# A hybrid DeltaNet and mLSTM layer on one core: gate functions and four kinds of transposition are issued a piece of the weight stream later

## The chip, the cores and the metric

The kernel runs on one core of a Trainium2 chip. The metric is the device time of one execution in microseconds (us), given as the median of three executions. The engines are named as in the profile: PE is TensorE (its matmuls; PEld are its weight loads), DVE is VectorE, ACT is ScalarE, POOL is GpSimd, SP is the queue from which all DMA transfers of this kernel start. Each engine takes its instructions strictly in the order in which the program issued them.

## The reference

One layer over 256 tokens of width 2048, all in float32. Two recurrent branches run side by side on the same normalised input and are merged by a gate for each channel:

```
h = RMSNorm_pre(x) * (1 + scale) + shift              # scale, shift, gate from c W_ada
[gdn_qkv | gdn_a, gdn_b | gdn_z | ml_qk | ml_v | ml_i, ml_f | ml_o | ml_z | g_A | g_B] = h W_in
y_A = W_pA( RMSNorm_head(GatedDeltaNet(conv(q, k, v), decay, beta)) * silu(gdn_z) )
y_B = W_pB( sigmoid(ml_o) * RMSNorm_head(mLSTM(conv(q, k), v, i, f)) * silu(ml_z) )
out = (sigmoid(g_A) * y_A + sigmoid(g_B) * y_B) W_out
x <- x + gate * RMSNorm_post(out)
```

The DeltaNet branch has 32 value heads, the mLSTM branch 8 heads of width 256. Both recurrences are computed from matmuls over the whole 256 tokens and a triangular inverse.

## The kernel before, in words

**The stream.** All weights pass through one object, `Stream`. A unit is one tile `raw` of 128 x 2048 floats (1 MB), three of which are kept in a ring. A unit is used in two **pieces** of 1024 columns. For a piece, `prep_w` writes two parts, the high part `whi` (a cast on ACT, line 169) and the remainder `wlo` (a subtraction, line 170, on DVE here; early in the kernel some on POOL). Four buffers of each are there. `mm3` (line 223) then makes each product of three matmuls: high by high, high by low, low by high. In most of the kernel a piece is 12 matmuls with 512 columns, or 24 with 256.

`Stream.run` writes the order of the work for all engines by hand. For piece i it issues the preparation of piece i + 3 (`ahead` is 3), then the matmuls of piece i, then, where the piece closes a group, that group's `after`, and then one `side.step()`. So in the queues of ACT and DVE the cast and the subtraction of piece i + 3 stand ahead of anything that follows from piece i. The cast of piece i + 4 needs the buffer that piece i frees.

**Side.** Everything that isn't a weight product is written as a generator in `Side` and goes on by one `yield` in each step, that is once in each piece. `wait(n)` lets n steps pass. Generators of rank 0 go first in a step, then those of rank 1 and 2. Instructions that a generator issues in step i stand on PE behind the matmuls of piece i and ahead of those of piece i + 1. PE works in order, so a transposition whose input isn't ready holds up the next piece. Steps that need PSUM tiles (`gtile`, four of them) ask with `banks` or `free` whether the tiles are free, and pass a step where they aren't.

**The first stage** (`BLOCKS`) computes 14 groups of 512 output columns in passes over parts of the contraction, since the input isn't complete yet. Each pass adds into the tiles `part` in SBUF. The last of these passes (contraction parts 12 to 15) sums up all 14 groups, two pieces for each. Its `after` adds the two PSUM tiles of the group on DVE (line 409), then applies on ACT a sigmoid (groups 0 to 8, 10 and 12) or SiLU (9, 11 and 13) over 128 x 1024 values (line 418), and stores the result in DRAM (`gate_dr`, line 420). For the odd groups from 9 on, DVE first multiplies it with the group before (line 422; store in line 423). After the last group `branches_open` drains the side work and hands the memory of this stage to the branches.

**The small gates** (`gates`, lines 450 to 511) run as side work from the start of that last pass: exponentials, logarithms and scans over 128 x 256 values for decay, beta and the mLSTM's input and forget gates. At their end PE transposes the two tiles `gt` and `g2` (lines 507 and 508) and ACT and DVE copy the result.

**The DeltaNet branch** takes eight periods of two head pairs (`gdn_period`, `zg` from 0 to 7). At the end of each, `gdn_stage2` scales the output `on` on DVE (line 879), waits two steps and transposes it (line 888) for the store `o_dr`.

**The mLSTM branch** takes four pairs of heads (`mlstm`, `m` from 0 to 3). For pair 0 alone the output gates arrive late: `gated_by` multiplies `hn` with the SiLU gate on DVE (`gate`, line 1023), passes one step, and goes on in `mlstm_out`, whose transpositions are line 992. For the other pairs `gated` does it with gates from DRAM.

**The output.** In two halves of 1024 columns, both branches' projections are summed in `py` tiles, `merge` multiplies and adds them on DVE and POOL (lines 1180 and 1181) into the tile `mg`, passes one step, and transposes `mg` 256 columns at a time (line 1190) into `m_hi` and `m_lo`. After the second half it also loads the rows of the last scale (`rws`), writes their product to DRAM (`bg_dr`, line 1206), reads it back broadcast (`bg`, line 1210) and loads the residual `xr` (line 1213). The product with `w_out` (`pw` tiles) and the last norm follow.

Of the kernel before, what the change touches and what calls it, by code (L numbers as in the profile page):

```python
# [9 lines left out]
AF = mybir.ActivationFunctionType  # L10
ALU = mybir.AluOpType
# [106 lines left out]
def hybrid_layer_kernel(  # L118
# [25 lines left out]
    V, A, T, G, SP = nc.vector, nc.scalar, nc.tensor, nc.gpsimd, nc.sync  # L144
# [80 lines left out]
    side = Side()  # L225
# [155 lines left out]
    def branches_open():  # L381

        nonlocal bp, x0, y0
        side.drain()
        st.close()
        bp = br.enter_context(tc.tile_pool(name="bp", bufs=2))

        x0 = bp.tile([P, 8, P], F32, name="x0", tag="x0", bufs=1)
        y0 = bp.tile([64, 8, 64], F32, name="y0", tag="y0", bufs=1)
        G.memset(x0, 0.0)  # L390
        G.memset(y0, 0.0)

    def add_start_groups(bi):

        groups, k0, nk = BLOCKS[bi][:3]
        lastb = bi == len(BLOCKS) - 1

        def use(g, ps, c, hi, lo, o):

            k = k0 + c  # L400
            h_chunks(k)
            for b in range(2):
                mm3(ps[b], h_hi[:, k, b * P:(b + 1) * P], h_lo[:, k, b * P:(b + 1) * P],
                    hi[:, o:o + 512], lo[:, o:o + 512], c == 0, c == nk - 1)

        def after(g, ps):
            for b in range(2):
                if k0:
                    V.tensor_tensor(part[g][:, b], ps[b], part[g][:, b], op=ALU.add)  # L409
                elif bi or g < 4 or b == 0:  # L410
                    A.copy(part[g][:, b], ps[b])
                else:
                    V.tensor_copy(part[g][:, b], ps[b])
            if bi == len(BLOCKS) - 2 and g == 3:
                late_consts()
            if lastb:
                pt = part[g].rearrange("p b c -> p (b c)")
                A.activation(pt, pt, AF.Silu if g in (9, 11, 13) else AF.Sigmoid)
                if g < 8:
                    SP.dma_start(gate_dr[g], part[g])  # L420
                elif g % 2:
                    V.tensor_tensor(part[g], part[g], part[g - 1], op=ALU.mult)
                    SP.dma_start(gate_dr[8 + (g - 8) // 2], part[g])
                if g == NG - 1:
                    branches_open()

        adders = []
        per = 1 if nk > 2 else 2
        for g in groups[::per]:
            st_ = {}  # L430

            def use_piece(h, hi, lo, g=g, st_=st_):
                for i in range(min(2, per * nk - 2 * h)):
                    gg, c = g + (2 * h + i) // nk, (2 * h + i) % nk
                    if c == 0:
                        st_["ps"] = [jtile(f"pn{i}") for i in range(2)]
                    use(gg, st_["ps"], c, hi, lo, i * 512)
                    if c == nk - 1:
                        after(gg, st_["ps"])
                    if bi == 0 and gg == NE - 2:  # L440
                        h_chunks(1)
                stream.ahead = 3 if bi else 1
            src = tuple(w_in[START[g + i]][:, k0 * 512:(k0 + nk) * 512] for i in range(per))
            adders.append(lambda src=src, use_piece=use_piece:
                          stream.add(src, lambda h, raw: prep_w(h, raw, per * nk * 512), use_piece,
                                     (per * nk + 1) // 2))
        return adders


    def gates(ps):  # L450
        gp = sp
        work = sp.tile([P, 2, D], F32, name="work", tag="xs").rearrange("p b (n s) -> p (b n) s", s=S)
        used = []

        def t_(n):
            used.append(n)
            return work[:, len(used) - 1]
        xb, ab, e, u, l, r = (t_(n) for n in ("xb", "ab", "e", "u", "l", "r"))
        V.tensor_scalar(xb, ps[:, 0:S], late_c["abb"][:, 0:1], None, op0=ALU.add)
        yield  # L460
        A.activation(ab, xb, AF.Abs)
        A.activation(e, ab, AF.Exp, scale=-1.0)
        na = gp.tile([32, 1], F32, name="na")
        A.activation(na, late_c["alog"], AF.Exp)
        yield
        G.tensor_scalar(u, e, 1.0, None, op0=ALU.add)
        yield from wait(2)
        A.activation(l, u, AF.Ln)
        A.activation(r, l, AF.Exp, scale=-1.0)
        yield  # L470
        G.tensor_scalar(u, u, -1.0, None, op0=ALU.add)
        G.tensor_tensor(e, e, u, op=ALU.subtract)
        G.tensor_tensor(e, e, r, op=ALU.mult)
        G.tensor_tensor(l, l, e, op=ALU.add)
        mn, sp_ = ab, u
        gt, g2, zz, on_, bf, bm, mm_ = (t_(n) for n in ("gt", "g2", "zz", "on_", "bf", "bm", "mm_"))
        G.memset(gt, 0.0)
        G.memset(g2, 0.0)
        G.memset(zz, 0.0)
        G.memset(on_, 1.0)  # L480
        yield from wait(2)
        V.scalar_tensor_tensor(mn, xb, 0.0, l, op0=ALU.min, op1=ALU.subtract)
        V.scalar_tensor_tensor(sp_, xb, 0.0, l, op0=ALU.max, op1=ALU.add)
        yield
        V.tensor_scalar(sp_[0:32], sp_[0:32], na[:, 0:1], -1.0, op0=ALU.mult, op1=ALU.mult)
        V.tensor_tensor_scan(bf[96:104], on_[96:104], mn[96:104], 0.0, op0=ALU.mult, op1=ALU.add)
        SP.dma_start(bm[64:72], bf[96:104])
        yield
        for b in range(2):
            c0, c1 = b * P, (b + 1) * P  # L490
            V.tensor_tensor_scan(gt[0:32, c0:c1], on_[0:32, c0:c1], sp_[0:32, c0:c1], 0.0,
                                 op0=ALU.mult, op1=ALU.add)
        A.activation(gt[32:64], mn[32:64], AF.Exp)
        yield from wait(2)
        V.tensor_tensor(gt[64:72], xb[64:72], bm[64:72], op=ALU.subtract)
        V.tensor_tensor_scan(mm_[64:72], zz[64:72], gt[64:72], 0.0, op0=ALU.add, op1=ALU.max)
        yield
        V.tensor_tensor(bm[64:72], bm[64:72], mm_[64:72], op=ALU.add)
        V.tensor_scalar(mm_[64:72], mm_[64:72], -1.0, None, op0=ALU.mult)
        yield  # L500
        A.activation(g2[64:72], bm[64:72], AF.Exp, scale=-1.0)
        SP.dma_start(rows[0:32], gt[0:32])
        SP.dma_start(rows[32:40], mm_[64:72])
        yield from wait(2)
        tp = gtile("tp")
        for b in range(2):
            T.transpose(tp[:, b * P:(b + 1) * P], gt[:, b * P:(b + 1) * P], ident)
            T.transpose(tp[:, S + b * P: S + (b + 1) * P], g2[:, b * P:(b + 1) * P], ident)
        A.copy(tt.rearrange("p a b -> p (a b)"), tp[:, 0:S])
        A.copy(tte.rearrange("p a b -> p (a b)"), tp[:, S:2 * S])  # L510
        V.tensor_scalar(ngt, tt[:, :, 0:32], -1.0, None, op0=ALU.mult)
# [85 lines left out]
    def wait(n):  # L597
        for _ in range(n):
            yield
# [156 lines left out]
    def gdn_stage2(zg, res, zr):  # L756
# [116 lines left out]
        for g, z, h, c in heads:  # L873
# [4 lines left out]
            for blk in range(2):  # L878
                V.scalar_tensor_tensor(ons[z][:, blk, h], ons[z][:, blk, h], so[:, z, blk, h:h + 1], sz[:, blk, c],
                                       op0=ALU.mult, op1=ALU.mult)  # L880
        yield from wait(2)
        yield from free(4)
        pts = [gtile(f"pt{z}", True) for z in range(2)]
        side.debt -= 0.8
# [99 lines left out]
    def mlstm_out(m, r):  # L984
        while "hn" not in r:
            yield
        hn = r["hn"]
        for h in range(2):
            pt = gtile("mpt")
            for cc in range(2):  # L990
                for b in range(2):
                    T.transpose(pt[:, cc * S + b * P:cc * S + (b + 1) * P], hn[h][:, b, cc * P:(cc + 1) * P], ident)
            hT = bp.tile([P, 2, S], F32, name="hT", tag=("qh", "ql")[h], bufs=1)
            for cc in range(2):
                ch = (2 * m + h) * 2 + cc
                A.activation(hT[:, cc], pt[:, cc * S:(cc + 1) * S], AF.Copy, scale=late_c["mnw"][:, ch:ch + 1])
            ch = (2 * m + h) * 2
            SP.dma_start(hb_dr[ch:ch + 2].rearrange("c d t -> d c t"), hT)
            yield

    def mlstm(m):
# [29 lines left out]
        def gated_by(sg, first):  # L1031
            while "hn" not in r or not (first or "gated" in r):
                yield
            for b in range(2):
                gate(b, sg[:, b], first)
            r["gated"] = True
            yield
            if not first:
                yield from mlstm_out(m, r)

        def gated():
# [128 lines left out]
    def merge(hf, yb):  # L1170
# [11 lines left out]
            yield  # L1182
        if hf == 0:
            load_gates(1)
        yield
        for k2 in range(hf * 4, hf * 4 + 4):
            ps = gtile("mtp")
            for kk in range(2):
# [195 lines left out]
```

## Time and profile before

| | us |
|---|---|
| median of three executions | 1620.76 |
| lowest and highest | 1618.08, 1620.88 |
| the profiled execution | 1616.79 |
| its span, first to last instruction | 1615.0 |
| busy: PE, DVE, ACT, POOL | 1585.7, 1148.3, 936.4, 235.2 |

All rows below are from the profiled execution, with times from the start of its span. A matmul's row lasts longer than the distance to the next one, since matmuls are pipelined: matmuls with 512 columns follow each other after about 0.23 us, though each lasts 0.39. So what PE loses in a stall is read from the distance of two starts, and it is a little more than the idle time that the profile names. In the rows of the chain of waits the three numbers are the total, the number of waits and the longest. In a row of the timeline they are start, duration, and behind the row in brackets the idle time before it with what ended it.

### The profile page before, as it was taken

To read this page: it belongs to the slowest core of one execution; us is meant where nothing else is said; L and a number is where in the kernel's file an instruction comes from. 1 tells how busy PE (TensorE), PEld (TensorE's weight loads), DVE (VectorE), ACT (ScalarE), POOL (GpSimd) and SP (SyncE) were. 2 spreads that over 40 slices of the span, in tenths; PEclk is the share of its full clock that TensorE was granted. 3 is DMA by queue.
4 is the path that set the end of the run, shared out by engine and by line. 5 is a ranking of instruction groups with operands and counts; after the bars stand their busy time and mean duration, and the time that the engine had idled before them with its cause. 6 is when DMAs were issued, how large, how long until landed. Compare 5 with 4: busy or idle time off the path is not lost.

```text
span 1615.0 us, 25449 instructions
## 1 busy us (share of the span) xinstructions
PE 1585.7 (98%) x9844; PEld 1388.1 (86%) x9844; DVE 1148.3 (71%) x1798; ACT 936.4 (58%) x1497; POOL 235.2 (15%) x191
## 2 busy tenths in 40 slices
PE   7999999899999999999999999999999999999998
PEld 4888888689999999999999999889988788888886
DVE  6685555675689878887888888776778556756654
ACT  7744445664666575757666666664665544444443
POOL 1787761000000000000000000000010000100100
PEclk9999999999999999999999999999999999999999
DMA  9898775665555546454646464557778668767573
GB/s 375 342 408 334 263 286 191 236 244 204 181 182 191 183 170 193 171 191 158 205 159 197 157 196 169 184 211 246 281 291 315 222 247 293 280 233 250 196 275 115
DMA packets 96261, 372.37 MB, mean 231 GB/s; under 512 B 26262, under 2 KB 46214, under 8 KB 58252
## 3 DMA queue, kind: packets, MB, share of 16 engines
q1 hardware_dynamic: 96140, 370.75, 64.5%
q8 instruction: 77, 1.26, 0.3%
q14 instruction: 44, 0.36, 0.1%
HBM read 354.40 MB, written 16.31 MB: 230 GB/s over the span
## 4 chain that ended last, share of the span: by engine, by line
PE 88%; DVE 3%; ACT 3%; issue 2%; DMA 2%; POOL 1%; SPq 0%; DVEq 0%; POOLq 0%; ACTq 0%
PE pn L223 31%; PE pt L223 29%; PE py L223 16%; PE pw L223 5%; ACT whi L169 2%; DVE wlo L170 1%; DMA raw<-in_dram 1%; DVE part L409 1%; PE psa L223 1%; DMA ar<-in_dram 1%; PE mz L808 1%; PE mq L799 1%; PE po L848 0%; PE pa L820 0%; PE pc L838 0%
## 5 line engine op out<-in xcount | busy, mean ns | idle before, releaser
L170 DVE TENSOR_TENSOR wlo<-raw,whi 128x1024 fp32r<-128x1024 f32 x454 | 560.6, 1245 | 266.6 <-ACT whi L169 265.4
L169 ACT CAST whi<-raw 128x1024 fp32r<-128x1024 f32 (+1 forms) x517 | 532.1, 1046 | 314.3 <-PE pn L223 148.8
L223 PE MATMUL pt<-h_hi,whi 128*128 128x256 f32 x1280 | 368.8, 288 | 0.0
L223 PE MATMUL pt<-h_hi,wlo 128*128 128x256 f32 x1280 | 363.0, 284 | 0.0
L223 PE MATMUL pt<-h_lo,whi 128*128 128x256 f32 x1280 | 362.8, 283 | 0.0
L223 PE MATMUL pn<-whi,h_hi 128*128 128x512 f32 x896 | 354.2, 395 | 7.9 <-ACT whi L169 5.8
L223 PE MATMUL pn<-wlo,h_hi 128*128 128x512 f32 x896 | 351.1, 392 | 3.3 <-DVE wlo L170 2.5
L223 PE MATMUL pn<-whi,h_lo 128*128 128x512 f32 x896 | 349.9, 390 | 0.0
L223 PEld LDWEIGHTS pt<-h_hi,whi 128*128 128x128 f32 x1280 | 246.0, 192 | 1.4
L223 PEld LDWEIGHTS pt<-h_lo,whi 128*128 128x128 f32 x1280 | 246.2, 192 | 0.3
L223 PEld LDWEIGHTS pt<-h_hi,wlo 128*128 128x128 f32 x1280 | 246.0, 192 | 0.0
L223 PEld LDWEIGHTS pn<-whi,h_hi 128*128 128x128 f32 x896 | 168.7, 188 | 45.7 <-ACT whi L169 6.2
L223 PEld LDWEIGHTS pn<-wlo,h_hi 128*128 128x128 f32 x896 | 168.7, 188 | 41.6 <-DVE wlo L170 7.4
L223 PEld LDWEIGHTS pn<-whi,h_lo 128*128 128x128 f32 x896 | 168.5, 188 | 35.3
L170 POOL TENSOR_TENSOR wlo<-raw,whi 128x1024 fp32r<-128x1024 f32 (+1 forms) x63 | 146.1, 2327 | 67.2 <-ACT whi L169 65.0
L223 PE MATMUL py<-whi,yhi 128*128 128x512 f32 x384 | 150.6, 392 | 0.0
L223 PE MATMUL py<-whi,ylo 128*128 128x512 f32 x384 | 149.6, 390 | 0.0
L223 PE MATMUL py<-wlo,yhi 128*128 128x512 f32 x384 | 149.5, 389 | 0.0
L409 DVE TENSOR_TENSOR part<-pn,part 128x512 f32<-128x512 f32 x112 | 73.5, 685 | 52.4 <-PE pn L223 52.4
L169 ACT CAST yhi<-ya 128x512 fp32r<-128x512 f32 x48 | 29.9, 622 | 131.7 <-PE py L223 129.0
L170 DVE TENSOR_TENSOR ylo<-ya,yhi 128x512 fp32r<-128x512 f32 x48 | 33.2, 691 | 91.3 <-ACT yhi L169 89.5
L585 DVE SCALAR_TENSOR_TENSOR qs<-pt,gcv,qs 128x255 f32<-128x255 f32 (+2 forms) x192 | 92.1, 480 | 4.6
(244 smaller groups left out, 1785.2 us busy)
## 6 DMA issues: line engine op xcount, KB each, us to landing
raw<-in_dram SPq DMA_DIRECT2D x259, 1024.0 KB
ar<-in_dram SPq DMA_DIRECT2D x32, 1024.0 KB
raw<-in_dram SPq DMA_DIRECT2D x16, 512.0 KB
ya<-o_dr SPq DMA_DIRECT2D x32, 256.0 KB
gate_dr<-part SPq DMA_DIRECT2D x11, 512.0 KB
gb<-rows SPq DMA_DIRECT2D x20, 256.0 KB
raw<-in_dram SPq DMA_DIRECT2D x6, 768.0 KB
ug<-ud SPq DMA_DIRECT2D x32, 128.0 KB
```

The source lines that it names most:

```text
L169: A.copy(hi, src)
L170: (eng or V).tensor_tensor(lo, src, hi.bitcast(F32), op=ALU.subtract)
L223: T.matmul(ps, l, r, start=start and i == 0, stop=stop and i == 2, skip_group_check=True)
L409: V.tensor_tensor(part[g][:, b], ps[b], part[g][:, b], op=ALU.add)
L585: V.scalar_tensor_tensor(dst[:, n, sh:], src[:, 0:S - sh], taps(n, 3 - sh), dst[:, n, sh:], op0=ALU.mult, op1=ALU.add)
L799: T.matmul(psp[64:128, m * 64:(m + 1) * 64], um(m)[0:64, 64:128], y0[:, m], start=True, stop=True)
L808: T.matmul(psz[0:64, m * 64:(m + 1) * 64], p2[64:128, m], x0[64:128, m, 64:128], start=True, stop=True)
```

## The change

Five steps are issued later, nothing is added or removed:

- The function (line 418), store and product of a group of the last summed pass move out of `after` into a generator `gate_values` of rank 0. The function comes one piece later (with the store, for groups 0 to 7), the product and its store two pieces later. For the last group `branches_open` drains the generator at once.
- `gates`: three steps instead of two before the transpositions of `gt` and `g2`.
- `gdn_stage2`: three steps instead of two before the transpositions of `on`, where `zg // 7` is 1, so for `zg` 7 alone.
- `gated_by`: one more step before `mlstm_out`, for pair 0 of the mLSTM.
- `merge`: two steps instead of one before the transpositions of `mg`, in both halves.

```
@@ add_start_groups, after
             if lastb:
-                pt = part[g].rearrange("p b c -> p (b c)")
-                A.activation(pt, pt, AF.Silu if g in (9, 11, 13) else AF.Sigmoid)
-                if g < 8:
-                    SP.dma_start(gate_dr[g], part[g])
-                elif g % 2:
-                    V.tensor_tensor(part[g], part[g], part[g - 1], op=ALU.mult)
-                    SP.dma_start(gate_dr[8 + (g - 8) // 2], part[g])
+                side.add(gate_values(g), 0)
                 if g == NG - 1:
                     branches_open()
+
+        def gate_values(g):
+
+            yield
+            pt = part[g].rearrange("p b c -> p (b c)")
+            A.activation(pt, pt, AF.Silu if g in (9, 11, 13) else AF.Sigmoid)
+            if g < 8:
+                SP.dma_start(gate_dr[g], part[g])
+            elif g % 2:
+                yield
+                V.tensor_tensor(part[g], part[g], part[g - 1], op=ALU.mult)
+                SP.dma_start(gate_dr[8 + (g - 8) // 2], part[g])
@@ gates
         SP.dma_start(rows[32:40], mm_[64:72])
-        yield from wait(2)
+        yield from wait(3)
         tp = gtile("tp")
@@ gdn_stage2
-        yield from wait(2)
+        yield from wait(2 + zg // 7)
         yield from free(4)
         pts = [gtile(f"pt{z}", True) for z in range(2)]
@@ gated_by
             r["gated"] = True
             yield
             if not first:
+                yield
                 yield from mlstm_out(m, r)
@@ merge
         if hf == 0:
             load_gates(1)
-        yield
+        yield from wait(2)
         for k2 in range(hf * 4, hf * 4 + 4):
             ps = gtile("mtp")
```

## The prediction

> **What bounds the kernel now.** I began with the page of the profile, then took the chain of waits of PE.
>
> ```profile
> PE 1585.7 (98%) x9844; PEld 1388.1 (86%) x9844; DVE 1148.3 (71%) x1798; ACT 936.4 (58%) x1497; POOL 235.2 (15%) x191
> ```
>
> ```profile
> PE pn L223 <- DVE wlo L170: 2.5, 6, 0.6
> PE mpt L992 <- DVE hn L1023: 1.8, 2, 1.5
> PE pn L223 <- DVE part L409: 1.6, 3, 0.7
> PE tp L508 <- ACT work L501: 1.1, 1, 1.1
> PE pt L888 <- DVE on L879: 0.7, 1, 0.7
> PE mtp L1190 <- POOL mg L1181: 0.6, 1, 0.6
> ```
>
> PE is busy for 98% of the span, so only what stalls PE is worth anything. The change moves the waiting side of most of these rows. Next I put a size on the stalls of the last summed pass. The windows give its balance, the rows of the tiles `pab` and `pt` say when PE ends the product before it and begins the one behind it, and the timeline gives one piece.
>
> ```profile
> 260.00:355.00 95.00, 90.12 (x421) 71.97 (x420) 59.42 (x72) 65.36 (x71) 5.65 (x10) 1.00 0.61 221
> ...
> L223 PE MATMUL pab<-h_hi,wlo x16: 280/283/284, 257.1 to 263.5; 128*128 128x256 f32 x16
> ...
> L223 PE MATMUL pt<-h_hi,whi x1280: 277/283/472, 348.2 to 1222.1; 128*128 128x256 f32 x183
> ...
> 269.08 0.39 PE L223 MATMUL pn<-whi,h_hi 128*128 128x512 f32 x1
> ...
> 271.80 0.39 PE L223 MATMUL pn<-whi,h_hi 128*128 128x512 f32 x1
> ```
>
> A piece takes 271.80 - 269.08 = 2.72 us. The pass has 28 of them: 76.2 us. It begins at 263.6 and ends where `pt` begins, at 348.2, so it takes 84.6. Four transpositions of the small gates belong to it, estimated at 0.4 from the 1.04 us of eight (a row further below). **The pass loses 84.6 - 76.2 - 0.4 = 8.0 us.** DVE (59 of 95 us) and ACT (65 of 95) aren't full in it, so it isn't their amount of work but its order. ACT and DVE show how it comes about:
>
> ```profile
> 275.94 1.06 ACT L418 ACTIVATE part<-part 128x1024 f32<-128x1024 f32 x1 [2.68 <-DVE part L409]
> 277.02 1.28 ACT L468 ACT_TABLE_LOAD   x1
> ...
> 278.75 1.28 ACT L469 ACT_TABLE_LOAD   x1
> ...
> 280.37 1.99 ACT L169 CAST whi<-raw 128x1024 fp32r<-128x1024 f32 x2
> ...
> 281.43 2.94 DVE L170 TENSOR_TENSOR wlo<-raw,whi 128x1024 fp32r<-128x1024 f32 x2 [5.53 <-ACT whi L169]
> 284.30 1.27 DVE L409 TENSOR_TENSOR part<-pn,part 128x512 f32<-128x512 f32 x2
> ...
> 319.36 1.06 ACT L418 ACTIVATE part<-part 128x1024 f32<-128x1024 f32 x1 [2.49 <-DVE part L409]
> ...
> 324.98 1.06 ACT L418 ACTIVATE part<-part 128x1024 f32<-128x1024 f32 x1 [2.67 <-DVE part L409]
> ...
> 321.39 2.36 DVE L170 TENSOR_TENSOR wlo<-raw,whi 128x1024 fp32r<-128x1024 f32 x2 [2.06 <-ACT whi L169]
> 323.67 1.28 DVE L409 TENSOR_TENSOR part<-pn,part 128x512 f32<-128x512 f32 x2
> ```
>
> Pieces are numbered from 0, so piece 2 begins at 269.08 and, with no stall, piece i ends at 266.3 + 2.72 i. At 277.02 the small gates put two functions with two table loads on ACT, and the two casts behind them start only at 280.37. These are pieces 7 and 8. The adds of group 2 (pieces 4 and 5, ended at 279.9) stand on DVE behind the subtraction of piece 8, so they run at 284.30, more than 4 us late. From there a circle keeps the delay alive: function, two casts, subtraction of the second, adds, next function. One turn of it is shown undisturbed from 319.36 to 324.98: **5.62 us, where PE needs 5.44 for two pieces.** It never catches up, and each later disturbance (two more exponentials of `gates`, each with a load and a load back) goes straight to PE.
>
> **The change part by part.** *Functions and products a piece later.* Nothing is added; the number of ACT, DVE and SP instructions stays. In the new order the cast of piece 2g + 5 stands ahead of the function of group g on ACT. The circle is then: function 1.06, one cast 1.0 (half of 1.99), its subtraction 1.23, adds 1.28, with some 0.2 for the handovers: 4.8 us against the 5.44 of PE. A delay now shrinks by 0.6 us per group. I followed the queues through the first half of the pass with these durations, the 1.28 us of a table load, and 0.4 us for each small function of `gates`. The two functions and loads of step 3 now come ahead of the function of group 1. They end at about 277.1, the cast of piece 7 at 278.1, its subtraction at 279.3; PE needs it at 282.9, where before it stalled. Group 1's function with its load back ends at 280.4, the subtraction of piece 8 at 282.7 (needed at 285.6), the adds of group 2 at 284.0 (their PSUM tiles are needed at 285.4). The exponential in step 8 comes when the delay is gone in good part: the subtraction of piece 12 ends at 293.8, needed at 296.4. The one in step 12 leaves the narrowest place: the adds of group 6 free their first PSUM tile at 305.7, needed at 307. So no stall of PE is left on paper, with 1 us of cover at the narrowest. The transpositions of the small gates run into the last exponential (the wait for L501 in the list); in the new order I have it done at 302.8, and they stand behind piece 15, at 307: no wait, with or without the third step. That 1.1 us wait is inside the 8.0 and isn't counted again. The products stand a piece behind their functions, so DVE doesn't wait for them; SP's stores now follow the loads that they stood ahead of, and the load due next comes two pieces later. The bounds: at best 8.0 comes back; at worst the disturbances go on to hit PE as the waits of the list say, and only the excess of the circle (0.18 us in 14 groups, 2.5) and the 1.1 come back: 3.6. I take **7.4**, near the top, since every place has cover.
>
> *`hn`, pair 0 of the mLSTM.*
>
> ```profile
> 1082.67 0.28 PE L223 MATMUL pt<-h_hi,whi 128*128 128x256 f32 x1
> ...
> 1085.54 0.60 PE L888 MATMUL pt<-con,on 128*128 128x128 f32 x4
> ...
> 1088.01 0.69 PE L773 MATMUL mp<-ycmp,au 32*32 32x32 f32 x32
> 1090.21 0.30 PE L992 MATMUL mpt<-con,hn 128*128 128x128 f32 x1 [1.51 <-DVE hn L1023]
> ...
> 1091.09 0.36 PE L223 MATMUL pt<-h_hi,whi 128*128 128x256 f32 x1
> ...
> 1095.63 0.21 PE L784 MATMUL mx<-pcm,xcmp 32*32 32x32 f32 x1
> ...
> 1089.65 1.42 DVE L1023 TENSOR_TENSOR hn<-hn,sg 128x256 f32<-128x256 f32 x4
> ...
> 1092.00:1095.50 3.50, 3.50 (x19) 3.41 (x17) 3.50 (x4) 1.15 (x2) 0.00 (x0) 0.53 0.62 164
> ```
>
> The `mp` matmuls end at 1088.70 and the next piece begins at 1091.09. Of these 2.4 us four transpositions are 0.4, so 2.0 is waiting for DVE. Then the granted clock falls to 0.53, and that piece takes 1095.63 - 1091.09 = 4.5 us where the piece at 1082.67 took 2.87: another 1.7. With the extra step that piece runs first, at about 1088.7 to 1091.6, and the transpositions behind it find `hn` done (1089.65 + 1.42 = 1091.07). DVE is full here, but its next subtractions are for pieces two and three ahead. I take 2.0 + 1.7 = **3.7**. The bounds: 2.0 if the clock falls all the same, 3.7 at the top.
>
> The Trainium skill ("TensorE: Matmul & The Clock Gate", section "What's actually happening") says that the PE clock falls to half after an idle window of about 3.4 us and comes back after a busy one. The 0.53 over 3.5 us fits that. The same page says that the window runs freely, so the wait for `on` ahead of it, which stays, could trip it on its own; by that this term is 2.0 and not 3.7.
>
> *`on`.* The seventh of eight groups of these transpositions waited (the one at 1085.54; 0.7 us in the list). The step is added for `zg` 7 alone, the eighth, and that ran without a wait:
>
> ```profile
> 1159.20 1.04 PE L888 MATMUL pt<-con,on 128*128 128x128 f32 x8
> ```
>
> So **nothing** is removed. The eight transpositions, two copies on ACT and two stores move by one piece; the store is read first in the output stage.
>
> *Merged columns.*
>
> ```profile
> 1393.10 0.27 PE L1190 MATMUL mtp<-con,mg 128*128 128x128 f32 x1
> 1394.00 0.55 PE L1190 MATMUL mtp<-con,mg 128*128 128x128 f32 x3 [0.63 <-POOL mg L1181]
> ...
> 1526.40 0.60 PE L1190 MATMUL mtp<-con,mg 128*128 128x128 f32 x4
> ```
>
> Two starts 0.9 us apart where 0.1 is usual: **0.8** comes back in the first half, nothing in the second, which doesn't wait. In the second half the chain behind it moves as well:
>
> ```profile
> 1545.20 0.31 SPq L1206 DMA_DIRECT2D bg_dr<-rws  x1
> ...
> 1549.49 0.34 SPq L1210 DMA_DIRECT2D bg<-bg_dr  x1
> 1549.93 0.38 SPq L164 DMA_DIRECT2D raw<-in_dram  x1
> ...
> 1561.13 1.05 ACT L169 CAST whi<-raw 128x1024 fp32r<-128x1024 f32 x1 [1.67 <-PE pw L223]
> ```
>
> SP stands still from 1545.5 to 1549.5, until the store has landed. A piece later this ends at 1552.2, and the weights due at 1549.93 go out at about 1552.6. Their first cast is at 1561.1, so 8.5 us are left: nothing lost, as long as they land within that.
>
> **The sum:** 7.4 + 3.7 + 0.0 + 0.8 = 11.9 us. The profiled execution took 1616.79, so its like would take 1604.9. It lies 4.0 under the median of the runs shown; the same gain from 1620.76 gives **1608.9**.
>
> **The rivals.** *A, the waits of the last pass move rather than go.* Then its term is the lower bound, 3.6, and the time 1620.76 - 3.6 - 3.7 - 0.8 = 1612.7. For it: all 14 functions and the loads of `gates` stay on ACT. Against it: ACT is at 65 of 95 us.
>
> *B, the mLSTM's gain is given back.* Behind the stall, weights arrive late:
>
> ```profile
> 1095.16 0.51 SPq L164 DMA_DIRECT2D raw<-in_dram  x1
> ...
> 1103.34 1.05 ACT L169 CAST whi<-raw 128x1024 fp32r<-128x1024 f32 x1 [1.86 <-DMA raw<-in_dram]
> ```
>
> A load from 1095.16 wasn't there before 1103.34, 8.2 us later. If PE runs 3.7 us ahead, it may meet such a load, or the clock falls again: the time is 1620.76 - 7.4 - 0.8 = 1612.6 at most. Against it: PE waits for none of these casts, which run two to three pieces ahead.
>
> *C, nothing comes of it:* the waits are taken over by others, and 1620.76 stays within 3 us.
>
> *D, slower.* SP issues in order and a store of the last pass waits for a function that now comes a piece later. If the weight loads behind it went out a piece late and their three-unit lead didn't cover it, each of some 13 loads could cost PE up to 2.72 us. The 4.5 us gained elsewhere are used up from 0.35 us per load; 1 us per load gives 1620.76 + 13 - 4.5 = 1629.3. For it: the loads share SP with these stores. Against it: no row shows PE or ACT waiting for weights in this pass, and DMA is busy 0.61 of it.
>
> **How the numbers follow.** The sum as forecast 0.68, A 0.10, B 0.12, C 0.06, D 0.04. What a measurement of this kernel tells from no change is about 0.2%, 3.2 us. The forecast, A and B lie beyond that on the fast side, with some doubt about the small ends: faster 0.88, within 0.08, slower 0.04. The range reaches from 1605, all bounds at the top (12.5) and the 3 us between single executions, to 1614.5, the two slower cases with a little more lost.
>
> **What would show it.** Right: the chain of waits of PE without `part`, `tp`, `mpt` and `mtp`, and with the 0.7 of `on`; `pt` beginning at about 340.8 where it began at 348.2; the functions (line 418) 5.4 to 5.6 us apart at most, the adds directly behind the group's last piece by the middle of the pass; no stretch at half clock near 1085. Wrong: PE rows with a wait for `wlo` in the last pass, a cast that waits for weights there, a granted clock near 0.5 behind `on`, or a `raw` load after 1552 that a cast waits for.

## The result, and the profile after

| | before | changed |
|---|---|---|
| median, us | 1620.6 (6 runs) | 1607.03 (6 runs) |
| lowest to highest | 1618.08 to 1620.88 | 1604.89 to 1608.65 |
| profiled execution | 1616.79 | 1608.11 |
| its span | 1615.0 | 1606.1 |

The ratio of the times is 0.9918, with a 95% interval of 0.9906 to 0.9931: the changed kernel is 0.8% faster, 13.6 us by the medians. The two profiled executions are only 8.7 us apart, because the one of before lies 3.8 us under its median and the one after 1.1 us over it. Where that comes from is part of the experiments.

The chain of waits of PE in the changed kernel (total, number, longest, in us). The first row here is from the start of the kernel, where nothing changed:

```profile
PE pn L223 <- ACT whi L169: 5.6, 1, 5.6
...
PE pnum L969 <- issue: 1.3, 1, 1.3
PE pt L894 <- DVE on L885: 1.0, 1, 1.0
...
PE pn L223 <- DVE wlo L170: 0.5, 1, 0.5
```

The rows for `part` on DVE, `tp`, `mpt` and `mtp` are gone. The wait for `on` is still there (line 879 of before is line 885 now). The wait of `pnum` is 1.3 where it was 0.6. That can't be put down to the change: the same row reads 0.5 to 1.3 in the profiles of the single parts below, and 0.7 in a second profile of the changed kernel.

The rows of the tiles `pab` and `pt` bracket the last summed pass again, and the timelines of ACT and DVE show the place where it went wrong before:

```profile
L223 PE MATMUL pab<-h_hi,wlo x16: 279/283/283, 257.3 to 263.7; 128*128 128x256 f32 x16
...
L223 PE MATMUL pt<-h_hi,whi x1280: 277/283/471, 340.5 to 1214.0; 128*128 128x256 f32 x183
...
277.20 1.04 ACT L169 CAST whi<-raw 128x1024 fp32r<-128x1024 f32 x1
278.26 1.28 ACT L425 ACT_TABLE_LOAD   x1
279.55 1.06 ACT L425 ACTIVATE part<-part 128x1024 f32<-128x1024 f32 x1
...
284.04 1.06 ACT L425 ACTIVATE part<-part 128x1024 f32<-128x1024 f32 x1 [1.54 <-DVE part L409]
...
288.53 1.06 ACT L425 ACTIVATE part<-part 128x1024 f32<-128x1024 f32 x1 [1.55 <-DVE part L409]
...
282.72 1.28 DVE L409 TENSOR_TENSOR part<-pn,part 128x512 f32<-128x512 f32 x2
```

The pass lasts from 263.8 to 340.5, **76.7 us instead of 84.6**. Its 28 pieces of 2.72 us and the four transpositions are 76.6, so nothing to speak of is lost any more. The cast of piece 7 now runs at 277.20, ahead of the function of group 1, where it came at 280.37. The adds of group 2 run at 282.72 and not at 284.30. The functions of groups 1, 2 and 3 follow each other after 4.49 us. That is one turn of the new circle: while there is a delay, each turn makes up 0.95 us on the 5.44 that PE needs.

The windows around the transpositions of `on`, cut where the granted clock changes. Behind the length of the window stand the busy times of PE, PEld, DVE, ACT and POOL, each with its number of instructions; then come the granted clock, the share of DMA and its GB/s:

```profile
1079.32:1082.73 3.41, 2.51 (x43) 2.03 (x44) 3.33 (x9) 3.40 (x6) 0.00 (x0) 1.00 0.61 173
1082.73:1086.14 3.41, 3.41 (x18) 3.41 (x18) 3.41 (x7) 2.16 (x4) 0.00 (x0) 0.50 0.34 139
```

The transpositions of `hn` don't wait any more, but 3.41 us at half clock followed all the same in this execution.

### The profile page after: what moved, and what is told of

Read it like the earlier page. It is cut to its first block, busy times and chain, and to the rows that moved or that the text cites. A ratio compares the mean times of both kernels' runs of the same rounds, so it can differ in the third digit from the quotient of the medians.

```text
span 1606.1 us, 25453 instructions
## 1 busy us (share of the span) xinstructions
PE 1582.6 (99%) x9844; PEld 1389.2 (86%) x9844; DVE 1146.9 (71%) x1798; ACT 938.2 (58%) x1497; POOL 234.4 (15%) x191
## 4 chain that ended last, share of the span: by engine, by line
PE 93%; DMA 2%; ACT 2%; DVE 2%; issue 1%; SPq 0%; POOL 0%; DVEq 0%; POOLq 0%; ACTq 0%
PE pn L223 35%; PE pt L223 28%; PE py L223 16%; PE pw L223 5%; DMA raw<-in_dram 1%; DVE wlo L170 1%; ACT whi L169 1%; PE psa L223 1%; DMA ar<-in_dram 1%; PE mz L814 1%; PE mq L805 1%; DMA gb<-rows 0%; PE pc L844 0%; PE po L855 0%; PE pt L894 0%
```

## The experiments

Each is compared with runs of the kernel before on its own chip.

### One part alone: the functions a piece later

The edit is the first hunk of the change and nothing else: `gate_values` as a side generator in place of the lines in `after`.

> The kernel before with one part of the change: the functions, products and stores of the last summed pass a piece later, all else as before. My theory (the circle of function, two casts, subtraction and adds takes 5.62 us where PE needs 5.44, and the new order takes one cast out of it): the pass shrinks from 84.6 us to about 77, the time falls by 7 to 8 us, and the wait of the small gates' transpositions goes as well although their step is not moved. Rival A (the waits move, they do not go): 3.6 us at most, and waits for wlo or tp stay in the pass.

Measured: 1610.41 against 1619.6 us, ratio 0.9945 (0.9932 to 0.9957), so 9 us with an interval of 7 to 11. The bracket of the pass:

```profile
L223 PE MATMUL pab<-h_hi,wlo x16: 279/283/283, 258.2 to 264.6; 128*128 128x256 f32 x16
...
L223 PE MATMUL pt<-h_hi,whi x1280: 277/283/562, 341.3 to 1215.7; 128*128 128x256 f32 x183
```

The pass takes 76.6 us. No wait for `tp` is in the list, although the small gates' transpositions are at their old step. This part alone makes two thirds of the gain. Rival A, 3.6 us, falls. Functions, products and stores moved together here, and no run takes them apart; the runs with a copy further down test the function's place.

### One part alone: the small gates' transpositions

```
         SP.dma_start(rows[32:40], mm_[64:72])
-        yield from wait(2)
+        yield from wait(3)
```

> The kernel before with the small gates' transpositions a piece later and nothing else. My theory: ACT and DVE set the pace of the pass, PE only waits elsewhere, at the next wlo: the wait of 1.1 us goes from the list, the pass stays at 84.6 us within 0.3, the time is the same. Rival (the waits of PE add up): 1.1 to 1.3 us faster.

Measured: 1619.37 against 1619.6 us, ratio 0.9998 (0.9989 to 1.0006). The wait for `tp` is gone, but the waits for `wlo` rose from 2.5 to 3.3 us in total, and the pass takes as long as before (265.2 to 350.0, 84.8 us):

```profile
310.99 0.50 PE L223 MATMUL pn<-wlo,h_hi 128*128 128x512 f32 x1 [0.56 <-DVE wlo L170]
313.62 0.27 PE L507 MATMUL tp<-con,work 128*128 128x128 f32 x1
...
314.48 0.47 PE L223 MATMUL pn<-whi,h_hi 128*128 128x512 f32 x1 [0.26 <-DVE part L409]
318.27 0.50 PE L223 MATMUL pn<-wlo,h_hi 128*128 128x512 f32 x1 [0.57 <-DVE wlo L170]
```

PE goes on past the transpositions and waits at the next pieces. A wait of 1.1 us in the list was worth nothing, since another pair of engines set the pace.

### The whole change without that part

The changed kernel with `wait(2)` in `gates`.

> The changed kernel with the small gates' transpositions at their old step. My theory: their input is ready by then in the new order, no wait for tp, the time stays within 0.5 us of the changed kernel. Rival: 1.1 us slower.

Measured: 1607.95 us, ratio to before 0.9937 (0.9916 to 0.9958), where the whole change has 0.9918. The intervals overlap widely, so by the time alone the 1.1 us of the rival would be possible as well. The pass settles it:

```profile
L223 PE MATMUL pab<-h_hi,wlo x16: 278/283/284, 257.9 to 264.3; 128*128 128x256 f32 x16
...
L223 PE MATMUL pt<-h_hi,whi x1280: 277/283/471, 341.1 to 1213.3; 128*128 128x256 f32 x183
```

It takes 76.7 us, as with the third step, and no row of PE waits for `tp`. So this hunk does nothing in either order.

### The circle, made longer in both orders

In both kernels the tile is copied onto itself behind the function, so its values stay the same and ACT has 14 copies more:

```
 A.activation(pt, pt, AF.Silu if g in (9, 11, 13) else AF.Sigmoid)
+A.copy(pt, pt)
```

> The kernel before with one copy more on ACT behind each function of the last summed pass (part onto itself, some 1.06 us, 14 of them; the values stay the same). My theory of the circle: one turn grows from 5.62 to 6.7 us, so the pass grows by 10 to 15 us and the time with it. Rival (the amount of work on ACT matters, 65 of 95 us): 80 of 95 us still fits, no change, under 2 us.

> The changed kernel with the same copy behind each function. My theory: the circle of the new order grows from 4.8 to 5.9 us, 0.45 over what PE needs, so the cover is used up late in the pass and some 2 to 6 us are lost, well under what the same copies cost in the old order. If the new order had taken the functions off the path altogether, nothing would be lost; if the functions were bound by the amount of work, as much as in the old order.

Measured with the order of before: 1635.26 against 1619.05 us, ratio 1.0102 (1.0086 to 1.0119), 16 us slower. Two functions in a row on ACT, and the bracket:

```profile
328.49 1.06 ACT L418 ACTIVATE part<-part 128x1024 f32<-128x1024 f32 x1 [2.49 <-DVE part L409]
...
335.20 1.06 ACT L418 ACTIVATE part<-part 128x1024 f32<-128x1024 f32 x1 [2.68 <-DVE part L409]
...
L223 PE MATMUL pab<-h_hi,wlo x16: 278/283/284, 258.6 to 265.0; 128*128 128x256 f32 x16
...
L223 PE MATMUL pt<-h_hi,whi x1280: 277/283/472, 362.8 to 1239.4; 128*128 128x256 f32 x183
```

One turn takes 6.71 us, about the 5.62 of before and one copy of 1.05. The pass grows by 13 us to 97.7, though ACT had room for the work. That is the circle, and not the amount of work: the same copies cost the pass 4.9 us in the new order, as follows.

Measured with the new order: 1614.01 us, ratio to before 0.9970 (0.9961 to 0.9979), against 0.9918 for the changed kernel: 0.5%, some 8 us, more than the 2 to 6 that I expected. The pass itself grew from 76.7 to 81.6 us; PE waits 1.4 us more behind it, for the casts and subtractions of its first `pt` pieces. The turn in the new order:

```profile
318.12 1.06 ACT L425 ACTIVATE part<-part 128x1024 f32<-128x1024 f32 x1 [1.00 <-DVE part L409]
323.70 1.06 ACT L425 ACTIVATE part<-part 128x1024 f32<-128x1024 f32 x1 [1.54 <-DVE part L409]
...
329.29 1.06 ACT L425 ACTIVATE part<-part 128x1024 f32<-128x1024 f32 x1 [0.24 <-DVE part L409]
```

5.59 us, where I had 4.8 + 1.05 = 5.85. It is the 4.49 us that the changed kernel shows without the copy, and the copy. The circle is still there in the new order; without the copy it is faster than PE. With it, its excess over PE is 0.15 us a turn, some 2 us in the whole pass. The other 2.9 of the 4.9 us are put down to the small functions of `gates` and their table loads, which lengthen single turns (to 7.44 us in two places) and which a circle slower than PE can't make up again; no run measures that share by itself. Of the 8 us, the pass and the waits behind it explain 6.3.

### One part alone: `hn` a piece later

```
             if not first:
+                yield
                 yield from mlstm_out(m, r)
```

> The kernel before with the extra step before mlstm_out of pair 0 and nothing else. The prediction's term: 3.7 us faster, no stretch at half clock. What the changed kernel's trace suggests instead: the wait of 2.0 us goes, the half clock behind it stays, since the wait for on ahead of it is enough to bring it; then 1.5 to 2.0 us faster, and a stretch of 3.4 us at a clock of 0.5 within 5 us of the transpositions of on.

Measured: 1615.74 against 1619.6 us, ratio 0.9974 (0.9965 to 0.9984): 4 us, with an interval of 3 to 6. The profiled execution has neither a wait at these transpositions nor one at `on`, and no half clock:

```profile
1080.00:1092.00 12.00, 12.00 (x149) 10.96 (x150) 11.23 (x25) 10.39 (x16) 0.00 (x0) 1.00 0.59 223
...
1092.17 0.66 PE L992 MATMUL mpt<-con,hn 128*128 128x128 f32 x4
```

The prediction's 3.7 lies in that interval; the 1.5 to 2.0 that I had set against it, with the half clock staying, does not. How both can be seen in one change is shown by the run with the small gates alone, where this stage is that of before. Its windows around the same place:

```profile
1088.48:1091.89 3.41, 1.73 (x37) 1.16 (x36) 3.33 (x9) 3.40 (x6) 0.00 (x0) 1.00 0.50 151
1091.89:1095.30 3.41, 2.34 (x10) 2.08 (x11) 3.41 (x7) 2.28 (x7) 0.00 (x0) 0.50 0.40 163
1095.30:1098.71 3.41, 3.41 (x18) 3.41 (x17) 3.05 (x3) 0.82 (x1) 0.00 (x0) 0.50 0.80 214
```

The half clock lasted two stretches there. In the first of them PE was busy for 2.34 of 3.41 us only, since it waited for `hn`; a second stretch followed. Of the five profiles in which `hn` is at its old step, three have one such stretch (the kernel before, the functions alone, the copy in the old order) and two have two (with `tp` alone, with the merged columns alone). Of the seven with `hn` moved and the rest of that stage as in the changed kernel or with `on` a step later, two have one and five have none. One stretch costs about half its length, 1.7 us. So the change removes the wait and on average also one stretch or a little more, but not in each execution.

The mean granted clock of the span, which is on record for every execution, says the same of many more executions (in the profiles the clock falls only here and in the last microseconds). On this chip it is 0.9967 on average in the 25 executions of before and 0.9983 in the nine with `hn` moved, but 0.9969 to 0.9972 in the runs with one of the other three parts alone. The 0.0016 between them are 2.6 us of 1616, or one and a half stretches; it is an estimate, since each value is rounded to 0.001. The time goes with it: on all chips together, the executions of before at 0.996 took 1619.0 to 1621.3 us, and the three at 0.999 took 1614.4 to 1615.1. In the pair of profiles that I compared, before had one stretch and so had after; hence 8.7 us there and 13.6 by the medians, at least for a part of the difference.

### One part alone: the merged columns a piece later

```
             load_gates(1)
-        yield
+        yield from wait(2)
```

> The kernel before with the transpositions of the merged columns a piece later and nothing else. The prediction's term: 0.8 us faster, which is at the edge of what can be told; the wait for POOL at mtp gone from the list, the second half unchanged, and no cast that waits for weights after the load of bg. Rival: the weights that go out 2.7 us later behind bg land too late, and PE waits for them near the end; then not faster.

Measured: 1617.96 against 1619.6 us, ratio 0.9991 (0.9981 to 1.0001). The time doesn't settle it: the 0.8 us of the forecast lie inside, and so does nothing at all. The trace shows the wait for POOL gone. The chain behind the second half, in the changed kernel:

```profile
1538.77 0.32 SPq L1213 DMA_DIRECT2D bg_dr<-rws  x1
1540.59 0.34 SPq L1217 DMA_DIRECT2D bg<-bg_dr  x1
1541.03 5.73 SPq L164 DMA_DIRECT2D raw<-in_dram  x2
```

SP stands still for 1.5 us until the store has landed, instead of 4.0 (why it lands sooner a piece later isn't shown), the weights go out at 1541.03, and no cast waits for weights from there to the end.

### Further: `on` a step later for `zg` 6 too

The forecast had it that the step is added to the wrong group. The edit to the changed kernel:

```
-        yield from wait(2 + zg // 7)
+        yield from wait(2 + zg // 6)
```

> The changed kernel with the extra step before the transpositions of on for zg 6 too, where the wait is (zg // 6 in place of zg // 7). My theory: the wait of 1.0 to 1.3 us for on goes, and with it the stretch of 3.4 us at half clock that it brings (1.6 us): 2.5 to 3.2 us faster than the changed kernel, and a granted clock of 1.0 there. Rival (the half clock has another cause, such as the many small matmuls of mp, or its window runs freely): 1.0 to 1.3 us faster, and a clock of 0.5 stays.

Measured: 1607.05 us, ratio to before 0.9931 (0.9916 to 0.9945): no gain over the changed kernel's 0.9918. My theory fell. The wait for `on` is gone, but PE now reaches the next side work at once and waits there longer:

```profile
1080.23 0.69 PE L779 MATMUL mp<-ycmp,au 32*32 32x32 f32 x32 [2.32 <-DVE ycmp L750]
...
1075.00:1080.00 5.00, 2.91 (x25) 2.71 (x23) 4.96 (x14) 4.36 (x8) 0.00 (x0) 1.00 0.39 143
```

DVE is busy for 4.96 of 5 us here. What it owes PE comes one behind the other, and a step later for one of them passes the wait to the next.

### Further: work of DVE issued earlier, and `vt`

Three kernels on one chip with the changed kernel as their measure. In the first, DVE scales `on` of `zg` 6 a step earlier, and `mp` of `zg` 7 comes a step later:

```
@@ ahead of mp
         res.update(xcmp=xcmp, ycmp=ycmp)
-        yield
+        yield from wait(1 + zg // 7)
@@ gdn_stage2, ahead of the scaling of on
-        yield from wait(2)
+        yield from wait(2 - (zg == 6))
@@ gdn_stage2, ahead of the transpositions of on
-        yield from wait(2 + zg // 7)
+        yield from wait(2 + zg // 6)
```

In the second, `pnum` of mLSTM pair 2 comes a step later:

```
         while "vt" not in r:
             yield
-        yield
+        yield from wait(1 + (m == 2))
```

> The changed kernel with the scaling of on for zg 6 a step earlier on DVE, where DVE stood idle for 3 us, its transpositions at their step as before, and the first matmuls of zg 7's second stage (mp) a step later. My theory: DVE is full for 10 us around this place (4.96 of 5 us in the run with on a step later, where the wait only moved to mp, 2.3 us), so only work issued earlier removes a wait: the waits for on and mp go, 1.0 to 1.5 us, and the half clock behind them (1.7 us) if the idle time is what brings it: 1.0 to 3.2 us faster than the changed kernel on the same chip. Rival (the wait moves once more, to wlo or hn): no change, and a wait of 1 us or more at another row near 1080.

> The changed kernel with one more step before the numerator matmuls (pnum) of mLSTM pair 2. My theory of the wait of 1.3 us there: weights land late, the cast that waits for them holds up the copy of vt behind it on ACT, and pnum needs vt; a piece later vt is there: the wait goes from the list, 1.0 to 1.5 us faster than the changed kernel. Rival (the late weights reach PE as well, rival B of the prediction): the next piece waits for wlo instead, no change.

> Both edits of the two runs before on top of the changed kernel. If both theories hold, the gains add up: 2.0 to 4.7 us faster than the changed kernel on the same chip; if the waits only move, no change.

> The changed kernel once more, on the chip of the three runs before and as their measure. The stretch at half clock behind on is expected to be 0, 3.4 or 6.8 us long from one execution to the next, since the same stage showed 3.4 us in one run, 6.8 in two others and none in a third; the time within 1605 to 1609.

| | median, us | ratio to before |
|---|---|---|
| changed kernel again | 1606.34 | 0.9917 (0.9903 to 0.9930) |
| `on` earlier, `mp` later | 1608.39 | 0.9926 (0.9913 to 0.9938) |
| `pnum` later | 1605.80 | 0.9917 (0.9904 to 0.9931) |
| both | 1607.96 | 0.9928 (0.9915 to 0.9940) |

None is faster than the changed kernel by more than can be told. With `on` earlier the waits for `on` and `mp` did go, and PE ran ahead, until it met late weights. ACT and PE of that run:

```profile
1094.65 1.04 ACT L169 CAST whi<-raw 128x1024 fp32r<-128x1024 f32 x1 [5.60 <-DMA raw<-in_dram]
1095.71 0.59 ACT L807 ACTIVATE p<-mq 64x512 f32<-64x512 f32 x1
...
1096.36 1.97 PE L814 MATMUL mz<-x,p 64*64 64x64 f32 x16 [2.06 <-ACT p L807]
...
1090.00:1096.00 6.00, 4.30 (x42) 3.94 (x40) 2.76 (x3) 1.33 (x2) 0.00 (x0) 1.00 1.02 406
```

DMA is full for these 6 us, at 406 GB/s. A cast waits 5.6 us for its weights, the copy of `p` stands behind it on ACT, and PE waits 2.1 us for `p`, with two stretches at half clock behind that. This is rival B's mechanism: in this profile, time won ahead of this place is given back to DMA. With both edits the same wait of PE for `p` is 2.4 us.

With `pnum` later, its wait (1.3 us in the changed kernel's profile, 0.7 in its second) is gone from the list. The second profile of the changed kernel shows no half clock behind `on`, as some executions were expected to. The profile names no releaser for that wait. What stands ahead of it on ACT in the changed kernel points to the late weights:

```profile
1189.50 1.05 ACT L169 CAST whi<-raw 128x1024 fp32r<-128x1024 f32 x1 [6.30 <-DMA raw<-in_dram]
1190.45 1.07 ACT L1015 COPY vt<-pn 128x512 f32<-128x512 f32 x2
```

The gain expected from it, 1.0 to 1.5 us, is not shown; 0.5 by the medians is inside the scatter. It stays open whether the wait went or only its row.

## Why the prediction was right, point by point

The time was 1607.03 where 1608.9 was forecast, inside 1605 to 1614.5.

- **The last summed pass** (7.4 of at most 8.0): right in size and in mechanism. The trace shows 7.9, the time of this part alone 7 to 11. The circle was shown by making it longer: one copy of 1.05 us in each turn cost 13 us in the pass in the old order and 4.9 in the new. The turn of the new order, worked out as 4.8, measures 4.49, so a delay shrinks by 0.95 us per group and not by 0.6. The queues followed on paper gave 278.1 as the end of the cast of piece 7 and 284.0 as the end of the adds of group 2; the profile has 278.2 and 284.0. Two signs came out otherwise at no cost: where loads of `gates` fall between two functions these stand up to 6.4 us apart from group 3 on, not 5.6, and one cast (at 317.02) waits 0.97 us for weights, which the prediction had as a sign of being wrong; PE waits for neither.
- **The small gates' transpositions** (nothing of their own): right. Alone they change nothing, and left out they aren't missed.
- **`hn`** (3.7, of it 2.0 wait and 1.7 half clock): the sum was right by the times of this part alone, 3 to 6 us. What failed is the assumption behind it, that the clock stays up once the wait is gone. "No stretch at half clock near 1085" was a sign of being right and "a granted clock near 0.5 behind `on`" one of being wrong; the changed kernel's profile shows the sign of being wrong, while another profile of it has a wait of 0.5 us for `on` and no fall. So the sum is right on average only, and that is partly luck: the one profile of before had one stretch, and its 1.7 us is not far from what goes on average. The Trainium skill ("TensorE: Matmul & The Clock Gate", section "What's actually happening") says that the window runs freely. My conclusion from it, that the waiting that is left may trip it, is borne out by two of the seven profiles.
- **`on`** (nothing): right that the step misses the group that waits. The run with the step at that group showed more: it would have been worth nothing there either. The step at `zg` 7 wasn't run alone; the other four parts alone make 9.2, 0.2, 3.9 and 1.6 us by the medians, more than the 13.6 of the whole, so no gain is left over that it would have to explain.
- **Merged columns** (0.8): the wait is gone; the time of this part alone, 0.9991 with an interval up to 1.0001, is too close to no change to confirm the size. The SP queue's detour cost nothing, as forecast, and was shorter than worked out.
- **Rival B** was not the way it went, but its mechanism shows in the profile of the run with `on` earlier, where late weights took what had been won. Rivals A, C and D fell.
- **The link from the profile to the median** was the weakest step. I took the profiled execution's 4.0 us under the median as something that stays. Its mean clock was 0.998 where before has 0.9967 on average, so perhaps 2 of these 4 us (an estimate from the rounded clocks) are a stretch or so at half clock that it happened not to have. The changed kernel's profiled execution came 1.1 us above its own median, and 1608.1 where the sum against the profile had 1604.9. The half clock that stayed is 1.7 of these 3.2 us and the wait of `pnum`, which scatters, 0.7. By the medians the gain was 13.6 and the sum 11.9. By the mean clocks the half clock gave some 0.9 more than the 1.7 counted, and the pass gave 0.5 more; both are estimates, and the little that is left stays open.

## What to carry to other kernels

Where two helper engines feed a third in a fixed order, add up one turn of the longest circle of instructions that wait for each other, and compare it with the time that the fed engine needs. Here it was 5.62 against 5.44 us, although both helpers were about a third idle. The excess by itself is 2.5 of the 8.0 us lost; the rest are delays (the function of group 2 came 9.67 us behind that of group 1) that a circle slower than PE can't make up again. Taking one cast out of the circle, by issuing the function one piece later, brought back all of it here; taking away a single wait of PE was worth nothing while the circle stood. And ahead of moving a waiting step, look at what the late engine owes next: in two runs here, with DVE full in one and DMA full in the other, the wait only changed its row.

## What the runs showed of the hardware

PE fell to half clock for whole stretches of 3.41 us, and a stretch of it followed a stretch in which PE was busy for part of the time. In nine profiles the 3.41 us just ahead of a fall show PE busy for 1.0 to 2.5 us, never idle throughout. In the run with `on` a step later a stretch of 3.41 us laid over its wait of 2.3 us shows 1.1 to 1.4 us of busy time, and the clock stayed up:

```profile
1076.50:1079.91 3.41, 1.41 (x12) 1.21 (x11) 3.41 (x9) 2.84 (x5) 0.00 (x0) 1.00 0.17 36
1077.50:1080.91 3.41, 1.09 (x37) 0.88 (x35) 3.33 (x10) 3.29 (x4) 0.00 (x0) 1.00 0.34 84
```

But these two need not be the stretches that decide. From the first fall to the last one, near the end of the kernel, there are 505.2, 518.8 or 522.2 us in the nine profiles, 148, 152 or 153 times 3.413. That points to a fixed grid. Counted back from the last fall of that run (1601.19), the two stretches of the grid over the wait are these:

```profile
1075.54:1078.95 3.41, 2.37 (x20) 2.17 (x19) 3.37 (x9) 2.79 (x5) 0.00 (x0) 1.00 0.28 118
1078.95:1082.36 3.41, 2.13 (x44) 2.12 (x45) 3.33 (x9) 2.70 (x5) 0.00 (x0) 1.00 0.78 267
```

The wait falls on both, and neither has less than 2.1 us of busy time. Still, the changed kernel fell behind a stretch with 2.51, so busy time alone doesn't part the falls from the rest; what does stays open. The same few microseconds of waiting cost 1.7 us more, or 3.4, or nothing, from one execution to the next, and a single profile can't tell which is typical. The Trainium skill ("TensorE: Matmul & The Clock Gate", section "What's actually happening") has windows of about 3.4 us that run freely, and the falls of exactly that length agree with it. Its idle window is not one without any matmul, as these rows show.
